# Hybrid decoder layer on one core: the first microseconds rearranged (early transposes on TensorE, an early table load, smaller first loads, other PSUM banks for the keys)

## Chip, core and metric

One Trainium2 chip, one of its cores. The metric is device microseconds for one execution of the whole kernel, the median of several runs. The engines have short names in the profile: PE (TensorE, matrix products), PEld (its weight loads), DVE (VectorE), ACT (ScalarE), POOL (GpSimd) and SP (SyncE, which here only issues DMA transfers).

## What is computed

A decoder layer on 1024 tokens of 1024 features: a SwiGLU half step, a mixer of three branches (a recurrence, sliding-window attention, attention into 256 memory tokens), and a second SwiGLU half step, each between RMS norms. What matters here is the beginning of the first half step, and the keys and values of the memory, which the kernel computes ahead of everything else:

```python
# memory: keys and values of 256 tokens
mem_n = rms_norm(mem, mem_norm_g)              # (256, 1024)
km, vm = split(mem_n @ w_kv, 2)                # 4 heads x 128 each
...
# first half step
f1 = swiglu(rms_norm(x, ffn1_pre_g), ffn1_w_in, ffn1_w_out)
h = x + 0.5 * rms_norm(f1, ffn1_post_g)
```

`rms_norm(t, g)` is `t * rsqrt(mean(t*t) + 1e-6) * g` along the features.

## The kernel before, in words

Everything lies with features on the 128 partitions and tokens along the free dimension; x is kept as 8 blocks of features by 2 halves of 512 tokens (`x[k][h]`, in the profile `acc`). Products of the layer proper use three matmuls per block with operands split into a high and a low part (`w_hi`, `w_lo` of a weight piece `w_raw`; lines 254 and 256 on ScalarE and VectorE; `u` and `r` for x, lines 379 and 380). A tile scheduler puts the instructions of each engine in order when the kernel is built; every engine then works through its own list strictly in that order. A few helpers (`keep`, here for transfers and matmuls of the opening) hold instructions in the order in which they are written.

The opening is `start()` (line 1018). Its order is written by hand:

- `send` (line 1022) issues a transfer on SP's queue. The order of the loads: memory (features 0 to 3, 512 KB), strip 0 of the key weights (512 KB), memory (features 4 to 7), strip 1, four blocks of x's first half (256 KB each), strip 2, the other four blocks of x. Strips have three buffers, so strip 3 waits until `keys(0)` has been computed, the first two strips of the value weights for `keys(1)` and `keys(2)`, the third for `keys(3)` and the last for `values(0)`. Between them are the first five pieces of the FFN weights (`w_raw`, 256 KB each) and the first four blocks of x's second half. SP's queue is in order too: a transfer that waits for its buffer holds all behind it. The transfers share eight semaphores in turn, so that a transfer also waits for the eighth before it.
- ScalarE scales the memory by its gain, one block at a time (line 1049, `mem_g`), and squares it (line 1071). Its first operation draws in a table load. The gain lies in `vecs`, a small load on ScalarE's own queue (line 1363).
- `keys(h)` (line 1055): 8 matmuls of 128x256 in full fp32, each of them two rows of the profile; two heads fill one PSUM bank `pk`. `values(s)` (line 1059): 4 matmuls of 128x512 (8 rows) into the two banks `pv`. Keys and values are computed from the scaled but not yet normalised memory; the factors 1/rms are applied afterwards to the keys (line 1103, `km`) and to the values (line 1110, `vm`).
- `rstd` (line 344) turns sums of squares into factors: PE sums over the partitions (`ps_ms`, line 351), VectorE computes twelve tiny steps (lines 356 to 367, `rsm`, `rsy`, `rsq`), and PE spreads the factors over the partitions (`ps_rs`, line 373). It is called for the memory, and inside that call, between its steps, for the first half of x (lines 1077 to 1085).

The order on PE that follows: keys(0), keys(1), keys(2), `ps_ms` of the memory, keys(3), `ps_ms` of x, values(0), `ps_rs` of x, `ps_rs` of the memory, values(1) to values(3), and then the first FFN product (`px`, line 512) of x's first half. Behind it come more of these products, during which x's second half is squared (lines 389 and 393), summed (`ps_ms`) and normalised.

PSUM has eight banks in two groups of four (line 338). `MAIN_PSUM` (line 35) lists the names that use the first group; every other name uses the second. `pq` (the name given to `pk` and `pv` in the opening), `px` and `py` are in the first group, `ps_ms` and `ps_rs` in the second.

Of the kernel before, what the change touches and what calls it, by code (L numbers as in the profile page):

```python
# [10 lines left out]
F32 = mybir.dt.float32  # L11
# [6 lines left out]
P = 128  # L18
# [3 lines left out]
KD = D // P  # L22
# [16 lines left out]
KH = KD // 2  # L39
# [38 lines left out]
class Block:  # L78
# [6 lines left out]
    def mm(self, *args, start=True, stop=True):  # L85
        return self.k.tc.keep_in_program_order(self.nc.tensor.matmul(*args, start=start, stop=stop))
# [114 lines left out]
class Builder:  # L201
# [639 lines left out]
    def rwkv_chain(self, pool, pk_d, inv_d, y):  # L841
# [7 lines left out]
        pairs = [(p, q) for p in range(NPAIR) for q in (0, 1)]  # L849
        keep = self.tc.keep_in_program_order  # L850
        mm = lambda *a, start=True, stop=True, **kw: keep(nc.tensor.matmul(*a, start=start, stop=stop, **kw))
        tile = lambda tag, shape, bufs=2: pool.tile([P] + shape, F32, tag=tag, name=tag, bufs=bufs)
        both = lambda x: x.rearrange("p a t -> p (a t)")
# [164 lines left out]
    def start(self, x, pool, km_d, vm_d):  # L1018
        nc, tc, io = self.nc, self.tc, self.io
        V = nc.vector  # L1020
        keep = tc.keep_in_program_order
        send = self.send = lambda *a: keep(nc.sync.dma_start(*a))
        mm = lambda *a, start, stop: keep(nc.tensor.matmul(*a, start=start, stop=stop))
        mem = pool.tile([P, KD, MEM], F32, name="mem_x", bufs=1)
        mg = pool.tile([P, KD, MEM], F32, name="mem_g", bufs=1)
        strips = []

        def load_mem(a):
            send(mem[:, a : a + KH], io["memT"][:, a : a + KH])

        def load_x(h, a):
            for k in range(a, a + KH):
                send(x[k][h], io["xT"][:, k, h * TH : (h + 1) * TH])

        def load_strip():
            n = len(strips)
            t = pool.tile([P, KD, P], F32, tag="mkv", name="mkv", bufs=3)
            send(t, io["mkv_k" if n < 4 else "mkv_v"][n % 4])
            strips.append(t)

        load_mem(0)
        load_strip()
        load_mem(KH)
        load_strip()
        load_x(0, 0)
        load_strip()
        load_x(0, KH)
        for k in range(KD):
            nc.scalar.activation(mg[:, k], mem[:, k], ACT.Copy, scale=self.vec("mem_norm_g", k))


        pk = [self.psum("pq") for _ in (0, 1)]
        pv = [self.psum("pq") for _ in (0, 1)]

        def keys(h):
            for k in range(KD):
                mm(pk[h // 2][:, h % 2 * MEM : (h % 2 + 1) * MEM], strips[h][:, k], mg[:, k], start=k == 0, stop=k == KD - 1)

        def values(s):
            w = strips[4 + s].rearrange("p b c -> p (b c)")  # L1060
            for a in (0, 1):
                k = 2 * s + a
                for i in (0, 1):
                    mm(pv[i], mg[:, k, i * P : (i + 1) * P], w[:, a * 512 : (a + 1) * 512], start=k == 0, stop=k == KD - 1)

        def mem_squares():
            out = []
            for a in (0, KH):
                sq = pool.tile([P, KH, MEM], F32, tag="mem_sq", name="mem_sq", bufs=1)
                s = pool.tile([P, MEM], F32, tag="mem_ss", name="mem_ss", bufs=2)  # L1070
                nc.scalar.activation(sq, mem[:, a : a + KH], ACT.Square)
                V.tensor_tensor(sq[:, :2], sq[:, :2], sq[:, 2:], ALU.add)
                V.tensor_tensor(s, sq[:, 0], sq[:, 1], ALU.add)
                out.append(s)
            return out

        def while_mem():
            keys(3)
            load_strip()
            self.factors_norm(x, HALVES[0], "ffn1_pre_g", pool, while_x, lambda k: self.factor_first(x, k))  # L1080

        def while_x():
            values(0)
            load_strip()
            self.prefetch(4, 0)

        self.fs = {"b11": [], "b21": []}
        sqs = mem_squares()
        keys(0)
        load_strip()  # L1090
        self.prefetch(2, 0)
        keys(1)
        load_strip()
        keys(2)
        load_strip()
        load_x(1, 0)
        ps, col = self.rstd(sqs, D, pool, MEM, True, between=while_mem)
        load_x(1, KH)
        rs = pool.tile([P, MEM], F32, name="mem_rs", bufs=1)
        nc.scalar.copy(rs, ps[:, :MEM])  # L1100
        for h in range(4):
            t = pool.tile([P, MEM], F32, tag="km", name="km", bufs=2)
            V.tensor_tensor(t, pk[h // 2][:, h % 2 * MEM : (h % 2 + 1) * MEM], rs, ALU.mult)
            nc.scalar.dma_start(km_d[:, h], t)
        values(1)
        values(2)
        values(3)
        for i in (0, 1):
            t = pool.tile([P, 512], F32, tag="mkv", name="vm", bufs=3)
            nc.scalar.activation(t, pv[i], ACT.Copy, scale=col[:, i : i + 1])  # L1110
            nc.scalar.dma_start(vm_d[:, i], t)
        self.send = nc.sync.dma_start
# [243 lines left out]
    def build(self):  # L1356
        nc, tc, io = self.nc, self.tc, self.io
        with contextlib.ExitStack() as outer, tc.tile_pool(reuse_waits="tile", name="consts", bufs=1) as cp, \
# [4 lines left out]
            nc.scalar.dma_start(self.vecs, io["vecs"])  # L1363
            self.ones = cp.tile([P, 1], F32, name="ones")
            nc.vector.memset(self.ones, 1.0)
            self.ident = cp.tile([P, P], F32, name="ident")
            nc.gpsimd.memset(self.ident, 1.0)
            nc.gpsimd.affine_select(self.ident, self.ident, [[1, P]], ALU.is_equal, 0.0, base=0, channel_multiplier=-1)
# [132 lines left out]
```

## Time and profile before

| | |
|---|---|
| time, median of 3 runs | 2378.74 us (2378.45 to 2380.33) |
| the profiled execution: its own time | 2381.53 us |
| span of that execution | 2379.8 us |
| transfers in the first 110 us | 24.27 MB, mean 221 GB/s |
| keys: 64 rows of PE up to 24 us | 16.6 us busy, mean 423 ns |
| values: 32 rows of PE up to 40 us | 14.1 us busy, mean 595 ns |

How to read it: the profile is one execution, with times from the start of its span. A row of the time line or of the chain gives a start, a length and what ran; "x48" are that many instructions merged. Matmuls overlap, so the distance between their starts and not the length of one is what each costs. A bracket such as `[0.87 <-ACT vm L1110]` says how long the engine had been idle before the row, and what ended it. A row of the waits gives the total, the number and the longest. A row of busy time by stretches gives the stretch, its length, the busy time and the number of instructions on PE, PEld, DVE, ACT and POOL, then the granted clock, the share of the DMA engines and GB/s.

### The profile page before, as it was taken

The page shows a single profiled execution, that of the slowest core. Times are in us where ns is not written, and L with a number is a line of the kernel's source. Part 1 is how long each engine was busy: PE and PEld are TensorE (multiplying, and loading weights), DVE is VectorE, ACT ScalarE, POOL GpSimd, SP SyncE. Part 2 cuts the span into 40 slices and gives each one's busy share as a digit, 9 for nine tenths or more (in the row PEclk, how much of TensorE's full clock was granted, in tenths as well). Part 3 has the DMA queues.
Part 4 walks back from the last instruction along what each step waited for, and adds up shares of the span by engine and source line. Part 5 has one row for each costly group of instructions (what it writes and reads, how often), then busy time and mean ns, then how long its engine had stood idle before and what let it go on. Part 6 is the DMA issues. An engine that isn't in the chain of part 4 may idle for free.

```text
span 2379.8 us, 33514 instructions
## 1 busy us (share of the span) xinstructions
PE 2343.9 (98%) x12388; PEld 1916.1 (81%) x12388; DVE 1543.4 (65%) x2584; ACT 891.6 (37%) x1648; POOL 95.5 (4%) x134
## 2 busy tenths in 40 slices
PE   8999999999999999999999999999999999999998
PEld 6788888888888777888868887778888888878888
DVE  6986555655478776894655456475998765564535
ACT  5423333422345444223454455234652233342211
POOL 0000000000000000001310000240000000000000
PEclk9999999999999999999999999999999999999999
DMA  7453222533244325325444324555545432263303
GB/s 277 136 188 121 86 87 80 178 115 106 97 161 142 110 99 189 135 93 175 144 156 153 123 97 150 185 188 166 174 162 183 156 120 82 83 202 100 114 23 107
DMA packets 196195, 323.80 MB, mean 136 GB/s; under 512 B 35360, under 2 KB 65568, under 8 KB 195776
## 3 DMA queue, kind: packets, MB, share of 16 engines
q1 hardware_dynamic: 180000, 294.33, 37.7%
q10 hardware_dynamic: 16032, 27.33, 3.4%
q8 instruction: 98, 1.61, 0.3%
q14 instruction: 65, 0.53, 0.1%
HBM read 231.41 MB, written 89.13 MB: 135 GB/s over the span
## 4 chain that ended last, share of the span: by engine, by line
PE 89%; DVE 5%; DMA 3%; ACT 2%; issue 1%; ACTq 0%; SPq 0%; DVEq 0%
PE po L317 7%; PE po L318 6%; PE po L319 6%; PE px L317 6%; PE px L318 6%; PE px L319 6%; PE pgate L317 4%; PE pgate L319 4%; PE pgate L318 4%; PE pz L317 3%; PE pz L318 3%; PE pz L319 3%; PE pr L319 2%; PE pr L317 2%; PE pr L318 2%; PE pb L318 2%
## 5 line engine op out<-in xcount | busy, mean ns | idle before, releaser
L254 ACT CAST w_hi<-w_raw 128x512 fp32r<-128x512 f32 x544 | 336.6, 621 | 903.0 <-PE po L318 213.1
L256 DVE TENSOR_TENSOR w_lo<-w_raw,w_hi 128x512 fp32r<-128x512 f32 x544 | 381.5, 702 | 183.0 <-ACT w_hi L254 171.7
L317 PE MATMUL po<-u,w_hi 128*128 128x512 f32 (+1 forms) x768 | 285.9, 372 | 0.9 <-DVE acc L627 0.9
L318 PE MATMUL po<-u,w_hi 128*128 128x512 f32 (+1 forms) x768 | 285.3, 372 | 0.0
L319 PE MATMUL po<-u,w_lo 128*128 128x512 f32 (+1 forms) x768 | 285.3, 372 | 0.0
L630 DVE TENSOR_TENSOR acc<-po,acc 128x512 f32<-128x512 f32 (+1 forms) x136 | 89.6, 658 | 162.6 <-PE po L319 162.0
L317 PEld LDWEIGHTS po<-u,w_hi 128*128 128x128 f32 x768 | 144.7, 188 | 26.3 <-DVE acc L627 1.6
L318 PEld LDWEIGHTS po<-u,w_hi 128*128 128x128 f32 x768 | 144.7, 188 | 24.9
L319 PEld LDWEIGHTS po<-u,w_lo 128*128 128x128 f32 x768 | 144.7, 188 | 25.0
L317 PE MATMUL pgate<-u,w_hi 128*128 128x512 f32 x384 | 152.8, 398 | 0.0
L319 PE MATMUL pgate<-u,w_lo 128*128 128x512 f32 x384 | 151.8, 395 | 0.0
L318 PE MATMUL pgate<-u,w_hi 128*128 128x512 f32 x384 | 150.0, 391 | 0.0
L317 PE MATMUL px<-f,w_hi 128*128 128x512 f32 x352 | 137.6, 391 | 3.1 <-ACT u L543 0.9
L317 PE MATMUL px<-u,w_hi 128*128 128x512 f32 x352 | 137.3, 390 | 1.2 <-ACT vm L1110 0.9
L318 PE MATMUL pz<-u,w_hi 128*128 128x512 f32 x352 | 137.2, 390 | 0.2 <-DVE u L380 0.2
L319 PE MATMUL px<-u,w_lo 128*128 128x512 f32 x352 | 137.2, 390 | 0.0
L317 PE MATMUL pz<-u,w_hi 128*128 128x512 f32 x352 | 137.0, 390 | 0.1
L319 PE MATMUL pz<-u,w_lo 128*128 128x512 f32 x352 | 137.0, 389 | 0.0
L318 PE MATMUL px<-u,w_hi 128*128 128x512 f32 x352 | 137.0, 389 | 0.0
L318 PE MATMUL px<-f,w_hi 128*128 128x512 f32 x352 | 136.9, 389 | 0.0
L319 PE MATMUL px<-f,w_lo 128*128 128x512 f32 x352 | 136.9, 389 | 0.0
L389 ACT ACTIVATE sq<-acc 128x512 f32<-128x512 f32 (+1 forms) x104 | 61.0, 598 | 93.2 <-DVE acc L630 75.7
(314 smaller groups left out, 4665.7 us busy)
## 6 DMA issues: line engine op xcount, KB each, us to landing
w_raw<-in_ffn_in SPq DMA_DIRECT2D x220, 256.0 KB
w_raw<-in_win SPq DMA_DIRECT2D x112, 256.0 KB
w_raw<-in_ffn_out SPq DMA_DIRECT2D x104, 256.0 KB
hid_d<-g SPq DMA_DIRECT2D x88, 256.0 KB
hid<-hid_d SPq DMA_DIRECT2D x88, 256.0 KB
gate_d<-gate SPq DMA_DIRECT2D x24, 512.0 KB
pk_d<-pk ACTq DMA_DIRECT2D x4, 2560.0 KB
f<-pk_d SPq DMA_DIRECT2D x16, 640.0 KB
```

What stands on the lines that cost most here:

```text
L254: self.nc.scalar.copy(hi, x)
L256: self.nc.vector.tensor_tensor(lo, x, hi.bitcast(F32), ALU.subtract)
L317: mm(out, wh, xh, start=first, stop=False, **kw)
L318: mm(out, wh, xl, start=False, stop=False, **kw)
L319: mm(out, wl, xh, start=False, stop=last, **kw)
L389: nc.scalar.activation(sq, x, ACT.Square)
L630: self.nc.vector.tensor_tensor(out, ps, out, ALU.add)
```

## The change

- Ahead of any data, PE does 16 transposes of the 128x128 identity into a PSUM tile `warm` that nothing reads. The identity is made by GpSimd (lines 1367 and 1368).
- ScalarE copies one column of ones into a tile `early` that nothing reads, right behind the issue of `vecs`; the table load now belongs to this copy.
- Memory and strip 0 are loaded in six pieces of 256 KB: memory 0 and 1, strip 0 blocks 0 to 3, memory 2 and 3, memory 4 and 5, strip 0 blocks 4 to 7, memory 6 and 7. Strip 1 and all that follows are as before.
- The two tiles of the keys have the name `pk` in place of `pq`, which isn't in `MAIN_PSUM`: they come from the second group of banks.

```diff
-        def load_mem(a):
-            send(mem[:, a : a + KH], io["memT"][:, a : a + KH])
+        def load_mem(a, b):
+            send(mem[:, a:b], io["memT"][:, a:b])
...
-        load_mem(0)
-        load_strip()
-        load_mem(KH)
+        warm = self.psum("warm")
+        for _ in range(16):
+            keep(nc.tensor.transpose(warm[:, :P], self.ident, self.ident))
+        strips.append(pool.tile([P, KD, P], F32, tag="mkv", name="mkv", bufs=3))
+        for a in (0, KH):
+            load_mem(a, a + 2)
+            send(strips[0][:, a : a + KH], io["mkv_k"][0][:, a : a + KH])
+            load_mem(a + 2, a + KH)
         load_strip()
...
-        pk = [self.psum("pq") for _ in (0, 1)]
+        pk = [self.psum("pk") for _ in (0, 1)]
         pv = [self.psum("pq") for _ in (0, 1)]
...
             nc.vector.memset(self.ones, 1.0)
+            nc.scalar.copy(cp.tile([P, 1], F32, name="early"), self.ones)
             self.ident = cp.tile([P, P], F32, name="ident")
```

The scheduler keeps the order of the engines as it was, but for these places in the opening: ScalarE scales six blocks of the memory ahead of the first squares instead of four, and casts one `w_hi` sooner; VectorE does four `w_lo` (line 256) ahead of the memory's first factor step `rsm` (line 356) and a fifth behind it, where before they stood between the factor steps; and some of `w_lo`, `u`, `r` and `km` change places between the factors and the first FFN products.

## The prediction

> **What bounds the kernel now.** I read the page from its top, then the chain that ended last, then the waits of PE, and only then the queues of the opening.
>
> ```profile
> span 2379.8 us, 33514 instructions
> ...
> PE 2343.9 (98%) x12388; PEld 1916.1 (81%) x12388; DVE 1543.4 (65%) x2584; ACT 891.6 (37%) x1648; POOL 95.5 (4%) x134
> ...
> PE 89%; DVE 5%; DMA 3%; ACT 2%; issue 1%; ACTq 0%; SPq 0%; DVEq 0%
> ```
>
> PE is the bound, and the whole change lies in the first 41 us of 2379.8. It can gain only what PE loses there. The chain of that stretch, in order of time (start, length, what):
>
> ```profile
> 0.81 4.00 DMA mem_x<-in_memT
> 4.88 1.28 ACT L1049
> ...
> 6.74 12.86 PE pq L1023 x48
> 19.59 0.79 PE ps_ms L351 x8
> 20.38 3.56 PE pq L1023 x16
> 23.94 0.79 PE ps_ms L351 x8
> 24.73 3.54 PE pq L1023 x8
> 28.27 0.41 PE ps_rs L373 x4
> 28.68 5.94 DMA w_raw<-in_ffn_in
> ...
> 40.78 0.50 PE px L317
> ```
>
> Here L1049 is the table load, the first pq the keys of heads 0 to 2, the second those of head 3, the third values(0); ps_ms are the sums of squares of the memory (first) and of x (second). At 28.27 the factors of x are spread over the partitions (ps_rs); at 40.78 the first FFN product starts. PE's waits up to 130 us (total, times, longest):
>
> ```profile
> PE pq L1023 <- ACT mem_g L1049: 6.7, 1, 6.7
> PE ps_ms L351 <- DVE sq L393: 1.2, 1, 1.2
> PE px L317 <- ACT vm L1110: 0.9, 1, 0.9
> PE px L317 <- DVE u L541: 0.7, 2, 0.4
> ```
>
> Three losses can be touched. The start, 6.7 us. A slow beginning: one head takes 3.56 us, so three should take 10.7, but they take 12.85 (6.74 to 19.59), 2.2 lost. And 0.9 us at px, which waits for a PSUM bank that values still held. If everything before 5 us is fixed by the loads, the most to be had is about 1.7 + 2.2 + 0.9 = 4.8 us, 0.2%.
>
> **The change part by part.** First what arrives when. The queue of SP, a row of ACT and one of DVE give landings, since each of these waited for an earlier load:
>
> ```profile
> 0.81 0.39 SPq L1022 DMA_DIRECT2D mem_x<-in_memT  x1
> ...
> 6.14 0.33 SPq L1022 DMA_DIRECT2D acc<-in_xT  x1
> 7.42 0.33 SPq L1022 DMA_DIRECT2D acc<-in_xT  x1
> ```
> ```profile
> 5.02 0.17 DVE L1370 TENSOR_SCALAR post<-vecs 128x8 f32<-128x8 f32 x1 [4.08 <-DMA vecs<-in_vecs]
> ```
> ```profile
> 4.00:8.50 4.50, 1.76 (x4) 1.49 (x5) 0.24 (x2) 3.61 (x6) 0.00 (x0) 1.00 1.02 412
> ...
> 15.00:19.50 4.50, 4.50 (x24) 3.96 (x22) 2.63 (x4) 3.46 (x6) 0.00 (x0) 1.00 1.03 382
> ```
>
> Memory's first half is there at 4.88 (its waiter is the table load), the first strip at 6.14, the second half at 7.42: 1.27 us for each 512 KB, with the 16 DMA engines full (share 1.02, 412 GB/s). In the same order and at the same rate, the six 256 KB pieces land 0.64 us apart: about 4.2, 4.9, 5.5, 6.1, 6.8, 7.4. The small vector load (vecs) is there at 5.0; ScalarE needs it for its scale, so the first scaled block starts at 5.0 even where the memory is earlier.
>
> ```profile
> 6.18 1.70 ACT L1049 ACTIVATE mem_g<-mem_x,vecs 128x256 f32<-128x256 f32 x4
> ...
> 7.79 1.04 ACT L1071 ACTIVATE mem_sq<-mem_x 128x1024 f32<-128x1024 f32 x1
> ...
> 17.37 1.28 ACT L254 CAST w_hi<-w_raw 128x512 fp32r<-128x512 f32 x2 [0.36 <-DMA w_raw<-in_ffn_in]
> 18.96 1.97 ACT L254 CAST w_hi<-w_raw 128x512 fp32r<-128x512 f32 x3 [0.30 <-DMA w_raw<-in_ffn_in]
> ```
>
> *Table load.* 1.28 us leave the chain: it now runs from about 1.2 us, under the loads. The early copy that draws it in is one column, under 0.2 us, before ScalarE has anything to do. Cost nothing; the cover is the wait to 4.88.
>
> *Pieces.* In the built order ScalarE now does six scaled blocks, the first squares, then two blocks (before: four, squares, four). Four take 1.70, so 0.40 apart: six from 5.0 to 7.4, squares to 8.35, the last two done by 9.25. At full clock a block of keys(0) takes 3.56 / 8 = 0.45 on PE, so keys(0) ends at 9.7, held by ScalarE and not by PE. Keys 1 and 2 add 2 x 3.56: 16.8 against 19.59, **2.8 us earlier**. The second strip (8.7 by the same spacing) is there by 9.7. SP issues three transfers more; at 0.39 each they end before 4.2, while over 1 MB is still on its way, so the queue doesn't run dry.
>
> *Transposes.* They need the identity and nothing else:
>
> ```profile
> 1.08 0.29 POOL L1368 TENSOR_SCALAR_AFFINE_SELECT ident<-ident 128x128 f32<-128x128 f32 x1
> ```
> ```profile
> L1303 PE MATMUL vtr<-ident,v_in x8: 271/273/273, 1323.5 to 1324.3; 128*128 128x128 f32 x8
> ```
>
> Eight of this size take 0.8 us (0.11 each) in mid-kernel. The slow rows of keys show about half speed at the start, so 16 take 1.8 to 3.7 us and end between 3.2 and 5.2: at or before the first scaled block (5.0 + 0.49 = 5.5). They cost nothing. The page's granted clock stands at 1.00 in this stretch (the figure ahead of the DMA share); only the rows show the slow start. Whether transposes end it no row of before shows: the bounds are all of the 2.2 us, or none. I take all; the rival prices none.
>
> *What is late next.* PE from 16.8: the rows from 19.59 to 28.27 are 8.7 us, so it could do ps_rs of x at 25.5. But VectorE computes the factors, and its built order changes: four w_lo now stand ahead of the memory's first factor step (rsm), a fifth right behind.
>
> ```profile
> 20.42 0.16 DVE L356 TENSOR_SCALAR rsm<-ps_ms 128x2 f32<-128x2 f32 x1 [2.48 <-PE ps_ms L351]
> ...
> 21.49 0.69 DVE L256 TENSOR_TENSOR w_lo<-w_raw,w_hi 128x512 fp32r<-128x512 f32 x1
> ```
> ```profile
> 24.76 0.16 DVE L356 TENSOR_SCALAR rsm<-ps_ms 128x4 f32<-128x4 f32 x1
> ...
> 25.45 0.16 DVE L361 TENSOR_SCALAR rsy<-rsm 128x4 int32<-128x4 int32 x1
> ...
> 27.43 0.16 DVE L367 SCALAR_TENSOR_TENSOR rsy<-rsq,rsy 128x4 f32<-128x4 f32 x1
> ```
>
> The fourth w_lo needs the fourth w_hi. The last three casts start at 18.96 because their data is only then there (382 GB/s, DMA share 1.03: full queues, which no earlier PE can hurry). Two of them end at about 20.25, w_lo to 20.95, rsm 0.2, the fifth w_lo 0.6, then the memory's chain 2.1 (25.45 to 27.59), x's rsm 0.2 and its chain 2.1: 26.2. For the smaller pieces I add 0.3: 1.6 MB at 382 GB/s, the rate seen where 256 KB transfers run alone, instead of 412 (4.1 us for 3.8). Bounds: 0 and, for a halved rate, 3.8. So ps_rs comes at **26.5**, PE idles 1.0 us ahead of it, and of 2.8 us only 28.27 - 26.5 = **1.8** is kept.
>
> *Banks.* Keys leave the four banks that px draws from; two are then free and the wait goes.
>
> ```profile
> 29.44 10.46 PE L1023 MATMUL pq<-mkv,mem_g 128*128 128x512 f32 x24
> ...
> 40.78 0.50 PE L317 MATMUL px<-u,w_hi 128*128 128x512 f32 x1 [0.87 <-ACT vm L1110]
> ```
>
> Values end at 39.9 before, 11.6 us after ps_rs began; so 38.1 now, and px follows at once: **0.87** more, 2.7 in all. Two things must be ready. The first four factors u ended with
>
> ```profile
> 37.54 0.68 DVE L380 TENSOR_TENSOR u<-acc,u 128x512 fp32r<-128x512 f32 x1
> ```
>
> and hang on w_raw pieces issued at 28.68, behind the last strip, which waits for values(0). That ends 2.4 to 2.8 us earlier, so u is there by about 35.8. In the other banks pk is held until km is read, while x's factors need two: the two that are left do.
>
> *Behind px.* The next loss is PE's 1.2 us ahead of the second half's sums:
>
> ```profile
> 49.29 0.59 ACT L515 COPY m<-px 128x512 f32<-128x512 f32 x1 [1.31 <-PE px L319]
> ...
> 59.26 1.02 PE L351 MATMUL ps_ms<-ones,sq 128*128 128x1 f32 x8 [1.17 <-DVE sq L393]
> ```
>
> ScalarE starts that run of work when PE ends a px (49.29), so it moves with PE; the 1.17 stays and the 2.7 is kept to the end. Sum: 1.8 + 0.87 = **2.7 us**. The profiled execution took 2381.53 (span 2379.8); the median run 2378.74, 0.1% less. Taken from the median: **2376.1**.
>
> **The rivals.**
>
> *The clock stays slow (the change doesn't do what it says).* Keys start at 5.5 instead of 6.74 and lose the same 2.2 again: keys end at 18.4, ps_rs at 27.1, and 1.2 + 0.87 = 2.0 us are gained: 2376.7; with a longer slow start up to 2377.9. For it: nothing in before shows a transpose on a cold PE. Against it: they are back-to-back work of 2 to 4 us. The Trainium skill, "TensorE: Matmul & The Clock Gate", Part 4 (PE-mode transpose), says that the full clock does not engage for transposes, which do not count as a busy PE in the same way; by that this rival is the case, and no run so far shows it.
>
> *VectorE does not hold.* The pieces come at least as fast as before, w_lo is through earlier, and ps_rs follows PE: 2.8 + 0.87 = 3.7, 2375.1; were the 1.2 us at 59 us to go as well, 4.8, 2373.9. Against it: the casts' wait at 18.96.
>
> *Given back at 59 us.* Were ScalarE's run held by the loads of w_raw or of x's second half, PE would wait longer there and nothing remain: 2378.7. Against: the 1.31 us that ScalarE waited for PE at 49.29.
>
> *Slower.* The pieces delay the stream, and w_lo, now in front of the factors, hands the delay on: each us that the fourth w_raw piece is late is one us at ps_rs. It turns into a loss from 26.2 + 2.9 = 29.1 on, a delay of 2.9 us (2.1 + 0.87 used up). At a halved rate, 3.8: 2379.6. Against: the x pieces have 256 KB already and ran with full queues. The Trainium skill, "DMA: Bandwidth & Descriptors", Bandwidth, asks for transfers of 1 MiB or more; by it the pieces would lose rate, which the 382 GB/s measured here largely denies.
>
> **How the numbers follow.** Forecast 50%, slow clock 18%, no hold at VectorE 14%, given back 10%, slower 8%. A measurement of this kernel tells 0.2% (4.8 us) from no change. Nearly all cases lie within that: faster by more needs the far end of the third case or a gain that I don't see, 9%; slower by more needs a delay of 7.7 us, 5%; so 86% between. Range: 2373.6 (the 4.8 us and a little) to 2380.0 (the loss of the last case).
>
> **What would show it.** Transposes from 1.5 us; the table load before 3; keys(0) from 5.5 with gaps on PE before its last blocks; keys rows at full pace from the start (or not, the first rival); the first rsm of VectorE behind w_lo at about 21; ps_rs at 26.5 after an idle PE; px with no wait for vm, near 38.1; ps_ms near 56.6 with its 1.2 us. Wrong if the pieces land further apart than 0.7 us, if px waits for u, or if the gap between 41 and 130 us grows.

## The result, and the profile after

The changed kernel took 2422.58 us (median of 4, 2420.34 to 2424.47) where the kernel before took 2378.59 (median of 4): a ratio of 1.018, interval 1.0168 to 1.0192. It is 44 us slower, and the forecast was 2.7 us faster. The page of the changed kernel begins:

```profile
span 2418.6 us, 33552 instructions
...
PE 2393.7 (99%) x12404; PEld 1918.8 (79%) x12404; DVE 1544.1 (64%) x2584; ACT 891.9 (37%) x1649; POOL 95.5 (4%) x134
```

PE is busy 49.8 us longer (2343.9 before), and the other engines hardly so (PEld by 2.7 us, VectorE by 0.7). The 16 transposes account for less than 4 us of that. So the opening comes first. The time line of the changed kernel (start, length, what, idle time before it):

```profile
1.25 1.28 ACT L1373 ACT_TABLE_LOAD   x1 [1.25 <-PEq L1493]
1.43 3.67 PE L1044 MATMUL warm<-ident 128*128 128x128 f32 x16 [1.43 <-POOL ident L1376]
...
4.58 0.91 ACT L1055 ACTIVATE mem_g<-mem_x,vecs 128x256 f32<-128x256 f32 x2 [1.84 <-DMA vecs<-in_vecs]
...
5.82 0.91 ACT L1055 ACTIVATE mem_g<-mem_x,vecs 128x256 f32<-128x256 f32 x2 [0.33 <-DMA mem_x<-in_memT]
...
6.92 0.91 ACT L1055 ACTIVATE mem_g<-mem_x,vecs 128x256 f32<-128x256 f32 x2 [0.20 <-DMA mem_x<-in_memT]
...
8.07 9.47 PE L1023 MATMUL pk<-mem_g,mkv 128*128 128x256 f32 x40 [0.17 <-DMA mkv<-in_mkv_k]
...
17.38 0.95 PE L351 MATMUL ps_ms<-ones,mem_ss 128*128 128x1 f32 x8
...
18.37 3.09 ACT L254 CAST w_hi<-w_raw 128x512 fp32r<-128x512 f32 x5 [1.01 <-DMA w_raw<-in_ffn_in]
...
21.46 0.15 DVE L356 TENSOR_SCALAR rsm<-ps_ms 128x2 f32<-128x2 f32 x1
...
26.65 1.58 PE L373 MATMUL ps_rs<-ident,rsy 128*128 128x128 f32 x12 [0.44 <-DVE rsy L367]
...
37.97 0.79 PE L317 MATMUL px<-u,w_hi 128*128 128x512 f32 x1
```

The table load is under the loads. The keys of three heads end at 17.4, VectorE holds PE at ps_rs (0.44 us), which begins at 26.65, and the first FFN product starts at 37.97 with no wait for a bank. All of this is close to the forecast (16.8, 26.5 and 38.1). The loads are not: the third, fourth and fifth piece of 256 KB let ScalarE and PE go on at 5.82, 6.92 and 8.07, where the forecast had 5.5, 6.1 and 6.8. At 38 us the changed kernel is 2.8 us ahead of the profile of before. It loses its time afterwards, and evenly. Two stretches in which PE never waits show it, in the kernel before (the first fence) and in the changed one (the second). The columns are the stretch, its length, PE's busy time with the number of matmuls in brackets, the granted clock, the share of the DMA engines, and GB/s.

```profile
540.00:600.00 60.00, 60.00 (x267) 1.00 0.30 98
```
```profile
540.00:600.00 60.00, 60.00 (x259) 1.00 0.36 117
```

Where 267 matmuls went through in 60 us, 259 do now: 225 ns from one to the next has become 232, at the same granted clock. (The counts include rows that reach over the ends of the stretch. From start to start, over all 128x512 rows of `u` with the weights `w_hi` and `w_lo` that follow each other without a wait, it is 227.0 ns before and 233.3 after.) The groups by line show which matmuls are slower. Before (the last two numbers ahead of the idle time are busy us and mean ns):

```profile
L319 PE MATMUL px<-u,w_lo 128*128 128x512 f32 x352 | 137.2, 390 | 0.0
...
L319 PE MATMUL po<-u,w_lo 128*128 128x256 f32 x128 | 36.2, 283 | 0.0
...
L1023 PE MATMUL pq<-mkv,mem_g 128*128 128x512 f32 x32 | 14.1, 595 | 0.0
```

and after:

```profile
L319 PE MATMUL px<-u,w_lo 128*128 128x512 f32 x352 | 139.4, 396 | 0.0
...
L319 PE MATMUL po<-u,w_lo 128*128 128x256 f32 x128 | 36.0, 281 | 0.0
...
L1023 PE MATMUL pq<-mkv,mem_g 128*128 128x512 f32 x32 | 14.1, 595 | 0.0
```

Only the layer's own matmuls of 128x512 with split operands (the dtype fp32r) are slower, by some 6 ns. Those of 256 columns are not, and neither are the full fp32 ones of the values, which take longer anyway. Of the 8,880 rows of 128x512 with split operands 8,688 are slower, so at 6.3 ns up to 55 us could be lost. PE's busy time rose by 46 us beside the transposes, and PE was idle 11 us less (35.9 us before, 24.9 after).

Three things that the change did to the whole kernel come into question:

- **S**: the tile `early` takes 32 bytes of SBUF (a column is padded to that), so everything allocated behind it on that side lies 32 bytes higher, the weights `w_hi` and `w_lo` among them. The moving operands (`u`, `r`) lie on the other side and stay. Products with both operands on the side that moves keep their distance, among them 192 rows with split operands (`pb` from `y`) and the fp32 ones of the values.
- **B**: `warm` is now the first PSUM tile, so the second group of banks gets banks 0 to 3 and the first group banks 4 to 7. They have changed places.
- **T**: sixteen transposes or the early table load make PE slower for the rest of the kernel.

The trace speaks against B already: before, `px` (banks 0 to 3) and `pz` (4 to 7) took 390 ns alike, and after, 396 and 396.

### The profile page after: what moved, and what is told of

Read it like the earlier page. It is cut to its first block, busy times and chain, and to the rows that moved or that the text cites. A ratio compares the mean times of both kernels' runs of the same rounds, so it can differ in the third digit from the quotient of the medians.

```text
span 2418.6 us, 33552 instructions
## 1 busy us (share of the span) xinstructions
PE 2393.7 (99%) x12404; PEld 1918.8 (79%) x12404; DVE 1544.1 (64%) x2584; ACT 891.9 (37%) x1649; POOL 95.5 (4%) x134
## 4 chain that ended last, share of the span: by engine, by line
PE 93%; DVE 2%; DMA 2%; ACT 1%; issue 1%; SPq 0%; ACTq 0%; DVEq 0%
PE po L317 7%; PE po L318 7%; PE po L319 7%; PE px L317 6%; PE px L319 6%; PE px L318 6%; PE pgate L317 4%; PE pgate L319 4%; PE pgate L318 4%; PE pz L319 3%; PE pz L318 3%; PE pz L317 3%; PE pr L317 2%; PE pr L319 2%; PE pr L318 2%; PE pb L318 2%
## 5 line engine op out<-in xcount | busy, mean ns | idle before, releaser
L317 PE MATMUL po<-u,w_hi 128*128 128x512 f32 (+1 forms) x768 | 289.7, 377 | 0.8 <-DVE acc L627 0.8
L318 PE MATMUL po<-u,w_hi 128*128 128x512 f32 (+1 forms) x768 | 289.2, 377 | 0.0
```

The source lines that it names most:

```text
L317: mm(out, wh, xh, start=first, stop=False, **kw)
L318: mm(out, wh, xl, start=False, stop=False, **kw)
```

## The experiments

**One suspect at a time, put into the kernel before.** 32 unused bytes behind the ones, and nothing else:

```diff
 nc.vector.memset(self.ones, 1.0)
+nc.vector.memset(cp.tile([P, 1], F32, name="pad"), 1.0)
```

> The kernel before with one unused column behind the ones (32 bytes), so that all later tiles on that side of SBUF lie 32 bytes higher, as in the changed kernel; banks, loads, transposes as before. Theory S (the shifted weights slow PE's fp32r rows): about 2425 us, and 259 PE rows in 540 to 600 us instead of 267. Theory B (the two groups of PSUM banks have changed places) and theory T (the transposes leave PE slower): about 2379 us, 267 rows.

Measured: 2421.64 us, one run (the kernel before beside it: 2380.38, median of 13).

```profile
540.00:600.00 60.00, 60.00 (x259) 1.00 0.37 119
```

So 32 bytes that nothing uses bring 41 us, nearly the whole slowdown. The same with `[P, 16]` (64 bytes):

> The kernel before with 64 unused bytes in the same place. If under theory S the place modulo 64 bytes counts: about 2379 us. If any shift against the tiles on the other side of SBUF counts: about 2425 us. Theories B and T: 2379 us.

2420.27 us, 259 rows: also slow, so the remainder modulo 64 is not what counts. The banks exchanged, by one transpose ahead of the loads:

```diff
+keep(nc.tensor.transpose(self.psum("warm")[:, :P], self.ident, self.ident))
 load_mem(0)
```

> The kernel before with a single transpose into a tile of the second PSUM group ahead of everything, so that this group gets banks 0 to 3 and the first group banks 4 to 7, as in the changed kernel; no shift in SBUF. Theory B: about 2425 us. Theories S and T (one transpose for sixteen): about 2379 us.

2379.89 us, 266 rows, with the same 2380.38 beside it. B has fallen. The reverse, the changed kernel with all of its opening and only the 32 bytes taken out:

```diff
-self.ones = cp.tile([P, 1], F32, name="ones")
+two = cp.tile([P, 2], F32, name="ones")
+self.ones = two[:, :1]
 nc.vector.memset(self.ones, 1.0)
-nc.scalar.copy(cp.tile([P, 1], F32, name="early"), self.ones)
+nc.scalar.copy(two[:, 1:], self.ones)
```

> The changed kernel, with the early copy written into a second column of the tile of ones, which takes no room: SBUF as before, all else of the change kept (transposes, pieces, banks, early table load). Theory S: the opening's gain alone is left, about 2376 us, 267 rows in 540 to 600 us. Theories B and T: about 2422 us, 259 rows.

2379.06 us (10 runs) against 2380.38 for the kernel before beside it, ratio 0.9997, interval 0.9987 to 1.0006. T has fallen too: transposes, pieces, banks and the early load are all in it, and the 44 us are gone. Of the 2.7 us of the forecast, though, 0.7 is left by this ratio, and the interval reaches from a gain of 3.1 us to a loss of 1.4.

**The cost by itself.** In the built kernels, and in bytes of a partition, `w_hi` starts at 27872 in the kernel before, 27904 and 27936 in the changed kernel and the one padded by 64 bytes, and the tiles `u` at 163808. Tiles of both kinds follow at 2048 bytes. 27872 and 163808 both leave 224 modulo 256; the other two starts leave 0 and 32. A kernel with no layer in it, only groups of 24 such matmuls, was to say whether this distance counts:

```diff
+def run(name, o, p, n=24):
+    ps = pmm.tile([P, TH], F32, tag="ps", name=name, bufs=4)
+    for j in range(n):
+        a, b = o + j % 4 * P, p + j % 4 * TH
+        keep(nc.tensor.matmul(ps, wt[:, a : a + P], ut[:, b : b + TH], start=j == 0, stop=j == n - 1))
...
+for p in [0, 8, 16, 24]:
+    for o in [8 * q for q in range(16)]:
+        run("u%dw%dz" % (p * 4, o * 4), o, p)
```

> The disputed cost by itself: no layer is computed, only 64 groups of 24 fp32r matmuls of 128x512 with nothing beside them; in each group the weights lie 0 to 480 bytes (steps of 32) from a place and the moving operand 0, 32, 64 or 96 bytes from one with the same remainder modulo 512; a group named u32w64z has the moving operand at 32 and the weights at 64. Theory R (what counts is the distance between weights and moving operand modulo 256 bytes, which is 0 in the kernel before and 32 and 64 in the slow ones): about 226 ns a matmul where u and w are equal modulo 256, about 232 ns elsewhere. Theory W (what counts is where the weights lie): the fast groups stand at the same w for every u. If neither PE alone nor the place makes it (a collision with other engines): all 64 groups alike.

Its time line, the first groups (start, length); a group's cost is the distance to the next start over 24:

```profile
19.75 5.61 PE L1375 MATMUL u0w0z<-ut,wt 128*128 128x512 f32 x24
25.20 5.75 PE L1375 MATMUL u0w32z<-ut,wt 128*128 128x512 f32 x24
30.79 5.76 PE L1375 MATMUL u0w64z<-ut,wt 128*128 128x512 f32 x24
36.39 5.77 PE L1375 MATMUL u0w96z<-ut,wt 128*128 128x512 f32 x24
42.00 5.76 PE L1375 MATMUL u0w128z<-ut,wt 128*128 128x512 f32 x24
```

u0w0: (25.20 - 19.75) / 24 = 227 ns. u0w32: (30.79 - 25.20) / 24 = 233. The groups with weights up to 288 bytes, in ns:

| weights at | 0 | 32 | 64 | 96 | 128 | 160 | 192 | 224 | 256 | 288 |
|---|---|---|---|---|---|---|---|---|---|---|
| moving at 0 | **227.1** | 232.9 | 233.3 | 233.7 | 233.3 | 233.3 | 229.6 | 232.9 | **227.1** | 232.9 |
| moving at 32 | 233.3 | **228.3** | 232.9 | 233.3 | 233.8 | 233.3 | 233.3 | 229.6 | 232.9 | **227.1** |
| moving at 64 | 229.2 | 233.3 | **226.7** | 233.3 | 233.3 | 233.3 | 233.7 | 233.3 | 229.6 | 232.9 |
| moving at 96 | 233.3 | 228.8 | 233.3 | **226.7** | 232.9 | 233.3 | 233.7 | 233.3 | 233.8 | 229.2 |

The fast place moves along with the moving operand and comes again after 256 bytes. A weaker one (229 to 230) lies 64 bytes below it. The rest is at 233 to 234, and the groups from 320 to 480 bytes repeat the pattern (the very last has no next start to measure by). It is the distance between weights and moving operand modulo 256 that counts (theory R), and PE shows it with next to nothing beside it: VectorE copies out one result per group, 0.69 us.

**Back in the layer.** Three kernels from the kernel before that tell the distance from the place:

```diff
+nc.vector.memset(cp.tile([P, 64], F32, name="pad"), 1.0)          # b_pad256, behind the ones
...
+rp = outer.enter_context(tc.tile_pool(reuse_waits="tile", name="rpad", bufs=1, side="right"))
+nc.vector.memset(rp.tile([P, 56], F32, name="pad_right"), 1.0)    # b_pad32r224, with the pad of b_pad32
...
+nc.vector.memset(rp.tile([P, 8], F32, name="pad_right"), 1.0)     # b_r32, with no other pad
```

> The kernel before with 256 unused bytes behind the ones: the weights lie 256 bytes higher, so that they and the moving operand are equal modulo 256 again. Theory R (the distance modulo 256 counts): about 2380 us and 267 PE rows in 540 to 600 us, though everything has moved. Any theory in which a shift as such costs: about 2421 us, 259 rows.

> The kernel before with the 32 bytes of the slow kernel on the side of the weights, and 224 unused bytes on the other side of SBUF, which put the moving operand 224 bytes lower: both are 0 modulo 256 then. Theory R: about 2380 us, 267 rows. Theory W (the place of the weights alone counts, and theirs is the slow one here): about 2421 us, 259 rows.

> The kernel before with its weights where they were, and the moving operand 32 bytes lower. Theory R: slow, about 2421 us, 259 rows. Theory W: 2380 us, 267 rows.

| kernel | weights mod 256 | moving mod 256 | us (one run) | PE rows in 540 to 600 us |
|---|---|---|---|---|
| before, beside them | 224 | 224 | 2376.89 | 267 in its profile above |
| 256 bytes more | 224 | 224 | 2377.20 | 266 |
| both sides moved | 0 | 0 | 2380.59 | 266 |
| moving operand alone moved | 224 | 192 | 2421.04 | 259 |

All three as theory R has it. The kernel in which the weights lie exactly where they were is the slow one:

```profile
540.00:600.00 60.00, 60.00 (x259) 1.00 0.35 118
```

The profile of the changed kernel has a comparison of its own. In `pb` the same weights meet moving operands of both kinds, `u` from the other side (now at a distance of 32) and `y`, which moved along with the weights and stayed at 0. Shortest, median and longest row in ns:

```profile
L318 PE MATMUL pb<-u,w_hi x128: 395/396/397, 1468.6 to 1575.6; 128*128 128x512 f32 x128
...
L318 PE MATMUL pb<-y,w_hi x64: 389/389/628, 1579.9 to 1623.8; 128*128 128x512 f32 x64
```

In the kernel before both medians are 389. (The rows of up to 628 lie in a stretch of lower granted clock, 0.83 from 1580 to 1590 us.) The values, too, kept their distance, so that their 595 ns don't tell whether full fp32 is free of the effect.

Last, the changed kernel itself, its early tile included, with 224 unused bytes on the other side:

```diff
+rp = outer.enter_context(tc.tile_pool(reuse_waits="tile", name="rpad", bufs=1, side="right"))
+nc.vector.memset(rp.tile([P, 56], F32, name="pad_right"), 1.0)
```

> The changed kernel as it is, its early column included, with 224 unused bytes on the other side of SBUF, which put the moving operand 224 bytes lower and so equal to the weights modulo 256 again. Theory R: about 2378 us, 267 PE rows in 540 to 600 us. If anything else in the change slowed PE: above 2400.

2374.66 us, 267 rows. The cause of the 44 us is settled by adding bytes as well as by removing them.

**What the opening is worth.** The transposes, in the changed kernel without its shift:

```diff
-for _ in range(16):
+for _ in range(1):
```

> The changed kernel without its shift in SBUF, and with one transpose in place of sixteen. If the transposes bring PE to full pace early, the keys of heads 0 to 2 end about 2 us later than with them (17.4 us in the changed kernel), near 19; if PE reaches full pace without them as well, near 17.4. At the first FFN product (38.0 with them) at most 1 us of it is left, since VectorE holds ps_rs there. Total 2376 to 2382 us in either case.

2373.56 us, one run (2376.89 before). The keys of three heads ended at 18.1 us with one transpose, 17.46 with sixteen; the first FFN product started at 38.01 and 38.35. So in this pair keys are later by 0.6 us without the transposes, which fits neither 2 us nor none, and at the FFN nothing is left of it. The other executions scatter as widely: keys ended at 17.38, 18.14 and 18.25 us with sixteen, at 18.56 with one. The edit also does more than it says: with one transpose the scheduler puts one `w_lo` ahead of the memory's first factor step and not four, so VectorE no longer holds ps_rs, and what the transposes bring the keys is not compared alone. Then both with more rounds:

> The changed kernel without its shift in SBUF, once more and with more rounds, for the worth of the opening alone. Old openings reached the first FFN product at 38.8 to 40.8 us in the profiles so far, this one at 38.0 to 38.4: about 1.3 us, 2378 where the kernel before takes 2379.5 (ratio 0.9994). If the forecast's 2.7 us hold: ratio 0.9989. If the slower clock seen at 55 to 66 us in its first profile belongs to it: ratio 1.000.

> The same with one transpose in place of sixteen. If the fifteen transposes are worth what the keys gain by them (0.6 us), this is 0.6 us slower than with them; if VectorE's hold of ps_rs takes that, equal; if its single time so far (3.3 us below the kernel before) is its own and not chance: ratio 0.9986, and it is the fastest version.

2375.49 and 2375.69 us (11 runs each) against 2377.65 (21 runs): both 0.9994, interval 0.9985 to 1.0003. Fifteen transposes, with the order that comes with them, make no difference to the total that can be seen, and the single 2373.56 lies within the range of the eleven (2373.01 to 2378.45). By these ratios, which go by means, the opening is worth some 1.4 us (0.06%), and the interval reaches from a gain of 3.6 us to a loss of 0.7, so that no gain at all is not excluded. No version is clearly faster than the kernel before.

Why it is nearer 1 than 2.7 can be read from the profiles. The old opening holds no product of split operands, so that the slow kernels count as well. In seven executions (one of them, b_banks, with a transpose ahead) it reached the first FFN product at 38.8, 38.9, 39.2, 39.4, 39.5, 40.7 and 40.8 us; the new one in six (two of them with a single transpose) at 38.0, 38.0, 38.3, 38.5, 38.6 and 39.0. The profile of before, from which the forecast took its terms, was the latest of all. The opening of the kernel with 256 unused bytes is at the other end:

```profile
6.41 12.12 PE L1023 MATMUL pq<-mem_g,mkv 128*128 128x256 f32 x48 [6.41 <-ACT mem_g L1049]
...
27.04 1.50 PE L373 MATMUL ps_rs<-ident,rsy 128*128 128x128 f32 x12
...
38.76 0.50 PE L317 MATMUL px<-u,w_hi 128*128 128x512 f32 x1
```

Its keys took 12.1 us instead of 12.9, they began 0.33 us sooner, and px did not wait for vm at all. Means of the two rows of numbers are 39.6 and 38.4, so 1.2 us.

The 1.2 us have two parts. From the start of the last three values to px it takes 9.90 us in each of the six new openings and 10.38 to 11.34 in the seven old, 10.65 in the mean: 0.75 us. The keys' other banks are the part of the change meant for this stretch; they were not tried alone. What lies ahead of it gained 0.45 us in the mean, where the forecast had 1.8. There the new opening loses to its loads. Before and after, up to 8.5 us:

```profile
1.00:8.50 7.50, 1.76 (x4) 1.00 0.86 323
```
```profile
1.00:8.50 7.50, 6.79 (x26) 1.00 0.86 270
```

The seven old openings moved 323 to 330 GB/s in this stretch, the six new ones 248 to 270, some 0.5 MB less by 8.5 us. The first cast of a weight piece, which waits for its load, starts at 17.0 to 18.0 us in the old and at 18.4 to 19.7 in the new. The early table load and the pieces are what the six have in common; b_banks, which has a transpose and neither of the two, moved 327. The pieces are the likelier cause, but neither was tried alone.

A part can be lost again behind px. The first profile of the changed kernel without its shift:

```profile
50.00:60.00 10.00, 8.83 (x42) 0.96 0.54 184
60.00:70.00 10.00, 10.00 (x44) 0.87 0.39 121
70.00:80.00 10.00, 10.00 (x46) 1.00 0.48 168
```

Behind PE's 1.2 us of waiting for x's squares the granted clock falls, 0.04 + 0.13 of 10 us, 1.7 us of full pace. It does so in four of the six executions with the new opening and in one of the seven with the old. All five are among the nine executions in which PE waited 1.17 us there; in the four slow kernels it waited 0.9 us, and the clock stayed at 1.00. Whether the new opening brings the dip on or chance does was not tried.

## Why the prediction was wrong, point by point

**The step that failed** is the one on the table load: "The early copy that draws it in is one column, under 0.2 us, before ScalarE has anything to do. Cost nothing". Its time was right (the table load from 1.25, the copy 0.19 us). What it left out is that a new tile also takes a place. Its 32 bytes moved the weights of every later product against their moving operands, from a distance of 0 modulo 256 to 32, and the rows from 227 to 233 ns: 41 us by b_pad32 alone, 44 by b_r32, where the moving operand moved and not the weights. None of the rivals had a mechanism that acts outside of the opening. The slower one of them was a delay of loads. Some of that came about, about 1 us at the first weight piece (18.37 for 17.37), where a loss needed 2.9. "Nearly all cases lie within" 0.2% rested on the same gap: the bounds were worked out for the first 41 us only.

The rest of the steps, by the opening of the changed kernel:

- *Table load, pieces, keys.* Right in kind: the load is out of the chain, and keys of three heads ended at 17.4 (16.8 forecast). "In the same order and at the same rate, the six 256 KB pieces land 0.64 us apart" was wrong: the third, fourth and fifth came 1.1 us apart, the rate from 1.0 to 8.5 us was 270 GB/s for 323, and the forecast's own sign of being wrong, pieces further apart than 0.7 us, came true. In the five later executions of this opening keys ended at 17.5 to 18.6.
- *VectorE holds ps_rs.* Right: its first factor step at 21.46 behind w_lo (21 forecast), ps_rs at 26.65 (26.5), PE idle there. The hold was mis-sized, 0.44 us for 1.0, because keys were later. With one transpose, and one `w_lo` ahead, PE didn't wait there at all.
- *The 2.7 us.* Right against the one execution it was worked out from (37.97 for 38.1), too large in general: 0.7 to 1.4 by the runs, none of it clear of noise. That 2.7 and the first profile's 2.8 agree is in part luck, since the base was the latest of seven. The terms that were mis-sized are the base and the pieces. The 0.87 us at px was 0 to 0.41 in the other old openings, and keys took between 12.1 and 13.6 us there.
- *The banks.* The wait for vm is gone in every new opening (none shows in four of the seven old ones either). The stretch up to px is 0.75 us shorter in the mean, close to the 0.87. That the two groups also changed places was not noticed, and cost nothing.
- *The slow clock.* The transposes did most of what the forecast took from them, and the rival failed in its mechanism. A key row takes 379 ns at full pace and some 630 while PE is slow. Of the first key rows 3, 0, 5 and 4 took over 600 ns in the four executions with sixteen transposes, 9 and 7 in the two with one, though keys began at the same 5.0 to 5.3 us, and 6 to 13 in the seven old openings. In the changed kernel the three slow rows still cost 0.8 us of the 2.2. The two extremes of the new opening up to 9 us, with sixteen and with one (shortest, median, longest):

```profile
L1023 PE MATMUL pk<-mem_g,mkv x12: 379/379/483, 5.3 to 8.8; 128*128 128x256 f32 x12
```
```profile
L1023 PE MATMUL pk<-mem_g,mkv x9: 634/634/795, 5.1 to 8.7; 128*128 128x256 f32 x9
```

The Trainium skill, "TensorE: Matmul & The Clock Gate", Part 4 (PE-mode transpose), holds that transposes don't bring the full clock. These rows speak against it. That the total doesn't show it (0.9994 both) fits what came next: keys at full pace waited for their strips (0.7 us in the changed kernel without its shift), and VectorE's order held ps_rs with sixteen (0.2 to 0.7 us) and not with one.

- *Given back at 59 us.* The 1.2 us ahead of ps_ms stayed (0.90 in the changed kernel) and moved with px, to 56.9 (56.6 forecast). What can be given back there is the clock behind it, which was no part of the rival.

The Trainium skill, "SBUF — State Buffer", Operand start alignment, asks only that an operand start at a multiple of its element size. These runs show that the time of an fp32r matmul hangs on more.

## What to carry to other kernels

A tile that nothing reads still moves every tile behind it: before costing an edit at nothing, compare the addresses of the matmul operands in the two built kernels, and not only the order of instructions. If every matmul of one shape is slower by the same few ns at a full granted clock, look there first, and try a pad in the old kernel, which costs one run. And take a term of some 2 us from several executions: one profile can be the end of a range as wide as the gain.

## What the runs showed of the hardware

- An fp32r matmul of 128x512 with its own weight load takes 227 ns where weights and moving operand are equal modulo 256 bytes in their partitions, 229 to 230 where the weights lie 64 bytes lower, 233 elsewhere (63 groups by themselves, in steps of 32 bytes); in the layer 227.0 and 233.3. Those of 256 columns show none of it (rows of 283 and 281 ns). Of full fp32 nothing is shown, since no such product came off or onto the fast distance. Why 256 bytes, and whether it is the weight load that collides with the stream, was not tried.
- Which of the two groups of PSUM banks a product uses made no difference to its pace (b_banks, 2379.89 us for 2380.38, 266 rows).
- Sixteen transposes before the first products shorten PE's slow start: 0 to 5 key rows of some 630 ns for 6 to 13 without them.
- After a wait of 1.2 us in dense work PE can run some 4 us at a granted clock near 0.6: 0.57 from 58 to 62 us in two of the profiles, and lower than 1.00 in five of the nine with that wait.
- With the first 1.5 MB in pieces of 256 KB the core moved 248 to 270 GB/s from 1.0 to 8.5 us, where it moved 323 to 330 before. The first scaled block came sooner (4.58 us, as soon as the gain was there), the first weight piece about 1 us later. Whether the pieces alone do it was not tried.
